# Two gate projections held until a block inversion has ended, its blocks read back over two DMA queues, and a residual scaling moved out of a merge loop

## The chip, the cores and the metric

The program runs on one core of one Trainium2 chip. The metric is the device time of one execution in microseconds. The core has a matrix engine (TensorE, PE in the rows; PEld is its loading of weights), three engines for elementwise work (VectorE or DVE, ScalarE or ACT, GpSimd or POOL), and SyncE (SP), which issues most DMA transfers. Each engine works through its own list of instructions in a fixed order; semaphores hold an instruction back until what it reads has been written.

## The reference, cut to what matters

The reference is three layers with different mixers and a product-key expert layer over 512 tokens of width 1024. The change lies in the third mixer, which runs a stick-breaking attention and a gated delta rule side by side and merges them through two gates:

```python
L = where(strict, einsum('bhnid,bhnjd->bhnij', k_beta, kc) * decay, 0)
T = triangular_solve(eye + L, eye)             # the inverse that the change is about
v_corr = T @ v_beta ; k_cumdecay = T @ (k_beta * exp(gc))
...                                            # scan over the chunks with these
o_gdn = rms_norm(o_gdn, gdn_out_norm_w) * silu(gdn_z)
merged = sigmoid(gate_sb) * y_sb + sigmoid(gate_gdn) * y_gdn
x = x + merged @ w_out
```

`gate_sb`, `gate_gdn` and `gdn_z` are projections of the layer's input. `x` on the last line is the output of a normalisation of the first block, so in the kernel it has still to be scaled by a gain per channel and a factor per token before anything is added to it.

## The kernel before, in words

Activations lie with channels on the 128 partitions and the 512 tokens along the free dimension, as 8 tiles. Every projection is done at nearly float32 accuracy in three products: `weights` (lines 197 to 212) brings a block of 128x1024 weights into `wraw` over the SP queue, ScalarE rounds it into `whi` (L207) and VectorE takes the rest, `wlo` (L208). The pool `wp` has **three buffers for each of `wraw`, `whi` and `wlo`**, shared by all projections. `proj_cols` (L220) then runs 24 matmuls of 512 columns on one PSUM bank of the tag `acc` (two banks): for each k of 8, whi with the high part, whi with the low part, wlo with the high part (L215, L216, L217).

The framework lists the instructions of each engine before the run: whatever is ready and has a free buffer is taken, earlier lines of the program first. Work that is written later thus fills gaps ahead of its place. A dependency of the kind `NoSync` sets this order alone; at run time nothing waits for it.

`gdn` (from L1205) goes through these stages:

- `stage1` for 8 heads makes `U[h]` (the matrices to invert) and stores their 32x32 diagonal blocks in DRAM (`ub`).
- `blocks()` (L1308 to L1320) loads all 128 diagonal blocks at once, one on each partition, inverts them on VectorE in 31 steps of a product (L1317) and a reduction (L1318), and stores them in DRAM (`xb`, L1320).
- `inverse(h)` (L1328 to L1360), run for two heads at a time, brings a head's inverted blocks back into `xd` (the tag `ld`, four buffers) with four DMAs (L1334) after a POOL memset (L1331), and joins them to the full inverse with products on PE (L1344, L1349, L1355, L1358), transposes (L1338, L1352), ScalarE copies (L1347, L1353, L1356) and VectorE operations (L1336, L1339, L1340, L1350, L1359). Its first product, L1344, is ordered behind `beside`, the ScalarE copy of gate tile 8.
- `gate_proj` (L1480) is one of 16 gate tiles (m = 0 to 15): a `proj_cols`, a ScalarE copy into `gp` (L1485) and a store (L1486). Tiles 0 to 8 are written ahead of the `inverse` calls, 9 to 13 between the four rounds of the scan, 14 and 15 behind it.
- `scan` and `finish` go over four rounds of 128 tokens and eight heads; `pair` (L541, its matmuls L556) starts the first two tiles of the next projection with the weights of `br_gdn`.
- `merge` (L1416) takes 8 tiles m: a sigmoid of the gates (L185 from `act`), a POOL product (L1422), the projection `br_gdn` on PE (tiles 2 to 7 in PSUM tag `sc`), a VectorE product and sum (L1425, L1426), the split into `mT` (L191 on ScalarE, L192 on VectorE), and then the scaling of the residual tile `xT[:, m]` (L1429), ordered behind that tile's L1426. The projection `mix_out` follows; its results are added to `xT` (L537).

Of the kernel before, what the change touches and what calls it, by code (L numbers as in the profile page):

```python
# [16 lines left out]
OP = mybir.AluOpType  # L17
AX = mybir.AxisListType
# [122 lines left out]
class Kern:  # L141
# [75 lines left out]
        mm(ps, ll, rh, start=False, stop=stop, **kw)  # L217
        return first

    def proj_cols(self, src, h, tag="acc"):  # L220

        hi, lo = self.weights(src, (8, 128))
        ps = self.ps(tag)
        for k in range(8):
            self.mm3(ps, hi[:, k], lo[:, k], h[0][:, k], h[1][:, k], k == 0, k == 7)
        return ps

    def proj_wide(self, srcs, h, tag="acc"):
# [976 lines left out]
    def gdn(self, ydram, sdram, xdram):  # L1205
# [3 lines left out]
        with ExitStack() as cx:  # L1209
# [99 lines left out]
            def blocks():  # L1309

                UB = p2.tile([128, 1024], F32, name="big", bufs=2).rearrange("p (a b) -> p a b", a=32)
                nc.sync.dma_start(UB, ub.rearrange("u b j i -> (u b) j i"))
                tb = p2.tile([128, 1024], F32, name="big", bufs=2)
                for j in range(30, -1, -1):
                    n = 31 - j
                    t = tb[:, :n * n].rearrange("p (m i) -> p m i", m=n)
                    nc.vector.tensor_mul(t, UB[:, j, j + 1:, None].to_broadcast([128, n, n]), UB[:, j + 1:, j + 1:])  # L1317
                    nc.vector.tensor_reduce(UB[:, j, j + 1:], t.rearrange("p m i -> p i m"), axis=AX.X, op=OP.add,  # L1318
                                            negate=True)
                nc.sync.dma_start(xb.rearrange("u b j i -> (u b) j i"), UB)  # L1320

            def four(fn):
                ps = self.ps("sc", (128, 4, 128))
# [4 lines left out]
            def inverse(h):  # L1328

                xd = p2.tile([128, 4, 128], F32, name="ld", bufs=4)  # L1330
                nc.gpsimd.memset(xd, 0.0)  # L1331
                for b in range(4):
                    r = slice(32 * b, 32 * b + 32)
                    nc.sync.dma_start(xd[r, :, r], xb[4 * h:4 * h + 4, b].rearrange("c j i -> j c i"))  # L1334
                td = p2.tile([128, 4, 128], F32, name="td", bufs=2)
                nc.vector.transpose(td.rearrange("p a b -> p (a b)"), xd.rearrange("p a b -> p (a b)"))  # L1336
                L = p2.tile([128, 2, 4, 128], F32, name="big", bufs=2)
                ps = four(lambda o, c: nc.tensor.transpose(o, U[h][:, c], self.ident))  # L1338
                nc.vector.tensor_mul(L[:, 0], ps, b4(l1))  # L1339
                nc.vector.tensor_mul(L[:, 1], ps, b4(l2))  # L1340
                yield
                P = p2.tile([128, 4, 128], F32, name="P", bufs=2)
                def first(o, c):
                    i = mm(o, L[:, 0, c], xd[:, c], start=True, stop=True)  # L1344
                    tc.add_manual_dep(i.ins, beside, nosync, reason="behind the gates")
                ps = four(first)
                nc.scalar.activation(P, ps, AF.Copy)  # L1347
                yield
                ps = four(lambda o, c: mm(o, td[:, c], P[:, c], start=True, stop=True))  # L1349
                nc.vector.tensor_sub(xd, xd, ps)  # L1350
                yield
                ps = four(lambda o, c: nc.tensor.transpose(o, xd[:, c], self.ident))  # L1352
                nc.scalar.activation(td, ps, AF.Copy)  # L1353
                yield
                ps = four(lambda o, c: mm(o, L[:, 1, c], xd[:, c], start=True, stop=True))  # L1355
                nc.scalar.activation(P, ps, AF.Copy)  # L1356
                yield
                ps = four(lambda o, c: mm(o, td[:, c], P[:, c], start=True, stop=True))  # L1358
                nc.vector.tensor_sub(U[h], xd, ps)  # L1359
                yield  # L1360
# [56 lines left out]
            def merge(p3, R2, ops):  # L1417
                mT = [pool.tile([128, 8, T], F32R, name="mT" + "hl"[z]) for z in range(2)]
                for m in range(8):
                    b, s = ops.pop(0) if ops else operands(p3, m)  # L1420
                    self.act(s, s, AF.Sigmoid)
                    nc.gpsimd.tensor_tensor(b, b, s[:, 0], op=OP.mult)  # L1422
                    ps = first[m] if m < 2 else self.proj_cols(A["br_gdn"][m], yT, "sc")
                    t = p3.tile([128, T], F32, name="mt", bufs=2)
                    nc.vector.tensor_mul(t, ps, s[:, 1])  # L1425
                    after = nc.vector.tensor_add(t, t, b).ins.name  # L1426
                    self.split(mT[0][:, m], mT[1][:, m], t)
                    x = self.xT[:, m]
                    i = nc.vector.scalar_tensor_tensor(x, x, self.fing[:, m:m + 1], R2, op0=OP.mult, op1=OP.mult)  # L1429
                    tc.add_manual_dep(i.ins, after, nosync, reason="behind the merge")  # L1430
                ss, add = self.sums("st")
                self.proj_part(A["mix_out"], rows(mT, 0, 8), self.residual(None, add), "acc", 2,
                               [A["peer_wq"][m] for m in range(2)])
                R = self.sm.tile([128, T], F32, name="R", bufs=1)
                self.rstd = []
                for half, hs in enumerate(HALVES):
                    self.rstd.append(self.rstd_x(ss, half))
                    self.rstd_rows(self.rstd[half], R, hs)
                    self.make_h(R, hs, self.fg)

            blocks()
            for m in range(9):
                beside = self.gate_proj(sdram, pool, m)
            for h in range(0, 8, 2):
                for _ in zip(inverse(h), inverse(h + 1)):
                    pass
# [4 lines left out]
            for c in range(4):  # L1451
                for g in range(4):
                    if g % 2 == 0:
                        raw = p2.tile([128, 4, 128], F32, name="xd", bufs=2)
                        ss = p2.tile([128, 4], F32, name="ss", bufs=3)
                    d = p2.tile([128, 2, 5, 128], F32, name="ld", bufs=4)
                    nc.sync.dma_start(d, gd[c, :, 2 * g:2 * g + 2])
                    for h in range(2):
                        scan(2 * g + h, c, d[:, h], raw, ss)
                    if g % 2:  # L1460
                        old.append((c, g // 2, raw, ss))
                    elif old:
                        finish(*old.pop(0))
                for m in ((9,), (10,), (11, 12), (13,))[c]:
                    self.gate_proj(sdram, pool, m)
            for m in range(14, 16):
                self.gate_proj(sdram, pool, m)
# [9 lines left out]
            nc.sync.dma_start(R2, xdram[:, 8])  # L1477
            merge(p3, R2, ops)

    def gate_proj(self, sdram, pool, m):  # L1480

        w = self.A[("gate_sb", "gate_gdn", "gdn_z")[m // 8]][m % 8]
        ps = self.proj_cols(w, self.hT)
        g = pool.tile([128, T], F32, name="gp", bufs=2)
        i = self.nc.scalar.activation(g, ps, AF.Copy)  # L1485
        self.nc.sync.dma_start(sdram[:, m // 8, m % 8], g)  # L1486
# [334 lines left out]
```

## Time and profile before

| | us |
|---|---|
| median of three runs | 2961.42 (2959.7 to 2961.81) |
| the profiled execution, its own time | 2964.76 |
| its span, first to last instruction | 2963.0 |
| PE busy in the span | 2827.3 (95%) |
| VectorE busy | 2135.7 (72%) |
| ScalarE busy | 1297.6 (44%) |
| POOL busy | 677.8 (23%) |

Times in the rows count from the span's start. In a timeline, a row gives start, duration, engine, line, operation, out<-in, shapes and how often; in brackets stands the idle time of the engine ahead of it and what ended that. An engine name with a q is its sequencer, as when it issues a DMA. The chain of work is followed back from the last instruction, so a stretch that is in it was waited for by what ended last.

### The profile page before, as it was taken

The page shows a single profiled execution, that of the slowest core. Times are in us where ns is not written, and L with a number is a line of the kernel's source. Part 1 is how long each engine was busy: PE and PEld are TensorE (multiplying, and loading weights), DVE is VectorE, ACT ScalarE, POOL GpSimd, SP SyncE. Part 2 cuts the span into 40 slices and gives each one's busy share as a digit, 9 for nine tenths or more (in the row PEclk, how much of TensorE's full clock was granted, in tenths as well). Part 3 has the DMA queues.
Part 4 walks back from the last instruction along what each step waited for, and adds up shares of the span by engine and source line. Part 5 has one row for each costly group of instructions (what it writes and reads, how often), then busy time and mean ns, then how long its engine had stood idle before and what let it go on. Part 6 is the DMA issues. An engine that isn't in the chain of part 4 may idle for free.

```text
span 2963.0 us, 43188 instructions
## 1 busy us (share of the span) xinstructions
PE 2827.3 (95%) x16320; PEld 2478.4 (84%) x16324; DVE 2135.7 (72%) x4184; ACT 1297.6 (44%) x2245; POOL 677.8 (23%) x550
## 2 busy tenths in 40 slices
PE   6999999999999999999889999999999999999989
PEld 5887887888789887777777888998999999999867
DVE  7566456676866554998666888977777777878885
ACT  2222234564755443775353435873333333333323
POOL 0101012110120000111011540005555553333350
PEclk9999999999999999999999999999999999999999
DMA  6453222211131224334363223779888888888773
GB/s 242 135 170 135 73 79 73 68 61 69 48 106 58 82 98 164 117 131 163 106 210 133 83 98 105 220 214 355 306 301 294 299 300 309 307 299 300 272 263 129
DMA packets 201008, 516.62 MB, mean 174 GB/s; under 512 B 27104, under 2 KB 79456, under 8 KB 198496
## 3 DMA queue, kind: packets, MB, share of 16 engines
q1 hardware_dynamic: 163504, 379.36, 37.2%
q0 software_dynamic: 36864, 134.23, 12.4%
q8 instruction: 128, 2.10, 0.3%
q14 instruction: 80, 0.66, 0.1%
q10 hardware_dynamic: 432, 0.27, 0.0%
HBM read 462.15 MB, written 51.64 MB: 173 GB/s over the span
## 4 chain that ended last, share of the span: by engine, by line
PE 69%; DVE 12%; issue 6%; ACT 5%; DMA 4%; POOL 4%; SPq 0%; POOLq 0%; DVEq 0%; ACTq 0%
PE pacc L215 8%; PE pacc L216 8%; PE pacc L217 8%; PE pst L216 5%; PE pst L215 5%; PE pst L217 5%; PE out L216 5%; PE out L217 5%; PE out L215 5%; DVE wlo L208 2%; POOL g L1742 2%; PE pacc L1670 2%; ACT whi L207 1%; PE ptr L1670 1%; DMA g<-in_peer_v_dram,ex 1%
## 5 line engine op out<-in xcount | busy, mean ns | idle before, releaser
L207 ACT ACTIVATE whi<-wraw 128x1024 fp32r<-128x1024 f32 x346 | 364.2, 1054 | 482.4 <-PE pacc L216 213.7
L208 DVE TENSOR_TENSOR wlo<-wraw,whi 128x1024 fp32r<-128x1024 f32 x325 | 407.2, 1254 | 230.8 <-ACT whi L207 225.1
L217 PE MATMUL pst<-hTh,wlo 128*128 128x384 f32 x1024 | 350.2, 342 | 1.7 <-DVE wlo L208 1.7
L215 PE MATMUL pst<-hTh,whi 128*128 128x384 f32 x1024 | 348.6, 340 | 1.0 <-ACT whi L207 1.0
L216 PE MATMUL pst<-hTl,whi 128*128 128x384 f32 x1024 | 348.8, 341 | 0.0
L215 PE MATMUL pacc<-whi,hTh 128*128 128x256 f32 x1216 | 341.0, 281 | 4.5 <-ACT whi L207 1.7
L216 PE MATMUL pacc<-wlo,hTh 128*128 128x256 f32 x1216 | 339.2, 279 | 0.0
L217 PE MATMUL pacc<-whi,hTl 128*128 128x256 f32 x1216 | 339.1, 279 | 0.0
L1742 POOL DMA_INDIRECT g<-in_peer_u_dram,ex x128 | 228.8, 1788 | 402.9 <-DVE w L1768 379.5
L217 PE MATMUL out<-whi,wl 128*128 128x512 f32 x768 | 305.2, 397 | 6.6 <-DVE wl L192 6.6
L216 PE MATMUL out<-wlo,wh 128*128 128x512 f32 x768 | 305.8, 398 | 4.7 <-DVE wlo L208 4.7
L215 PE MATMUL out<-whi,wh 128*128 128x512 f32 x768 | 305.1, 397 | 0.0
L207 ACT ACTIVATE whi<-vr 128x1024 fp32r<-128x1024 f32 x126 | 133.5, 1060 | 275.9 <-PE pst L216 245.7
L1742 POOL DMA_INDIRECT g<-in_peer_v_dram,ex x128 | 180.8, 1412 | 257.7 <-DVE w L1768 230.8
L215 PEld LDWEIGHTS pacc<-whi,hTh 128*128 128x128 f32 x1216 | 228.9, 188 | 5.9 <-ACT whi L207 1.9
L217 PEld LDWEIGHTS pacc<-whi,hTl 128*128 128x128 f32 x1216 | 229.1, 189 | 0.6
L216 PEld LDWEIGHTS pacc<-wlo,hTh 128*128 128x128 f32 x1216 | 228.9, 188 | 0.5
L215 PE MATMUL pacc<-hTh,whi 128*128 128x512 f32 x560 | 221.2, 395 | 1.8 <-DVE old L1132 1.2
L217 PE MATMUL pacc<-hTh,wlo 128*128 128x512 f32 x560 | 221.9, 396 | 0.2 <-DVE wlo L208 0.2
L216 PE MATMUL pacc<-hTl,whi 128*128 128x512 f32 x560 | 221.7, 396 | 0.0
L191 ACT ACTIVATE wh<-w 128x384 fp32r<-128x384 f32 x128 | 67.1, 524 | 340.8 <-PE out L216 274.5
L215 PEld LDWEIGHTS pst<-hTh,whi 128*128 128x128 f32 x1024 | 192.9, 188 | 7.0 <-ACT whi L207 1.3
(646 smaller groups left out, 6551.0 us busy)
## 6 DMA issues: line engine op xcount, KB each, us to landing
wraw<-in_peer_ut_dram SPq DMA_DIRECT2D x128, 512.0 KB
vr<-in_peer_v_dram SPq DMA_DIRECT2D x126, 512.0 KB
gd<-big SPq DMA_DIRECT2D x24, 1024.0 KB
gg<-gd SPq DMA_DIRECT2D x16, 1536.0 KB
wraw<-in_mod_w_dram SPq DMA_DIRECT2D x32, 512.0 KB
wraw<-in_ret_vg_dram SPq DMA_DIRECT2D x32, 512.0 KB
wraw<-in_gdn_qkv_dram SPq DMA_DIRECT2D x24, 512.0 KB
gd<-pk SPq DMA_DIRECT2D x8, 1280.0 KB
```

The costliest lines, as they stand in the source:

```text
L191: nc.scalar.activation(hi, src, AF.Copy)
L207: i = self.nc.scalar.activation(hi, raw, AF.Copy)
L208: j = self.lo.tensor_tensor(lo, raw, hi.bitcast(F32), op=OP.subtract)
L215: first = mm(ps, lh, rh, start=start, stop=False, **kw)
L216: mm(ps, lh, rl, start=False, stop=False, **kw)
L217: mm(ps, ll, rh, start=False, stop=stop, **kw)
L1670: end = mm(ps[:, i], o2[:, i], o1[:, i], start=True, stop=True).ins.name
L1742: i = nc.gpsimd.indirect_dma_start(out=g, out_offset=None, in_=A["peer_u" if up else "peer_v"], in_offset=bass.IndirectOffsetOnAxis(ap=ex[ ...
```

## The change

Four edits, all in `gdn` and its helpers:

- `blocks()` returns the name of its last reduction. `gate_proj` and `proj_cols` take it as `after`: the first matmul of gate tiles 6 and 7 is ordered behind that reduction (NoSync).
- Gate tile 8 is no longer written ahead of the inverses but in the first round of the scan, with 9. `beside` is thereby the copy of tile 7, so L1344 comes behind tile 7.
- Of the four DMAs that bring a head's blocks back, those of b = 0 and 2 are issued from ScalarE's queue, the others from SP's as before.
- In `merge` the scaling of `xT` gets a loop of its own behind the merge loop; `after` is then the sum of tile 7 for all eight.

```diff
-    def proj_cols(self, src, h, tag="acc"):
+    def proj_cols(self, src, h, tag="acc", after=None):
...
-            self.mm3(ps, hi[:, k], lo[:, k], h[0][:, k], h[1][:, k], k == 0, k == 7)
+            m = self.mm3(ps, hi[:, k], lo[:, k], h[0][:, k], h[1][:, k], k == 0, k == 7)
+            if after and k == 0:
+                nosync = mybir.DependencyInfo(mybir.DependencyClass.NoSync, mybir.DependencyReason.SCHED_ONLY)
+                self.tc.add_manual_dep(m.ins, after, nosync, reason="kept for later")
...
-                    nc.vector.tensor_reduce(UB[:, j, j + 1:], t.rearrange("p m i -> p i m"), axis=AX.X, op=OP.add,
-                                            negate=True)
+                    i = nc.vector.tensor_reduce(UB[:, j, j + 1:], t.rearrange("p m i -> p i m"), axis=AX.X, op=OP.add,
+                                                negate=True)
                 nc.sync.dma_start(xb.rearrange("u b j i -> (u b) j i"), UB)
+                return i.ins.name
...
-                    nc.sync.dma_start(xd[r, :, r], xb[4 * h:4 * h + 4, b].rearrange("c j i -> j c i"))
+                    q = nc.sync if b % 2 else nc.scalar
+                    q.dma_start(xd[r, :, r], xb[4 * h:4 * h + 4, b].rearrange("c j i -> j c i"))
...
                     self.split(mT[0][:, m], mT[1][:, m], t)
+                for m in range(8):
                     x = self.xT[:, m]
                     i = nc.vector.scalar_tensor_tensor(x, x, self.fing[:, m:m + 1], R2, op0=OP.mult, op1=OP.mult)
                     tc.add_manual_dep(i.ins, after, nosync, reason="behind the merge")
...
-            blocks()
-            for m in range(9):
-                beside = self.gate_proj(sdram, pool, m)
+            inverted = blocks()
+            for m in range(8):
+                beside = self.gate_proj(sdram, pool, m, inverted if m > 5 else None)
...
-                for m in ((9,), (10,), (11, 12), (13,))[c]:
+                for m in ((8, 9), (10,), (11, 12), (13,))[c]:
...
-    def gate_proj(self, sdram, pool, m):
+    def gate_proj(self, sdram, pool, m, after=None):
...
-        ps = self.proj_cols(w, self.hT)
+        ps = self.proj_cols(w, self.hT, after=after)
```

## Rows read from the trace of the kernel before

**Rows 1.** Waits of PE, 1350 to 1650 us: who, for what, total, times, longest.

```profile
PE psc L1344 <- DMA ld<-xb: 7.6, 1, 7.6
PE psc L215 <- ACT whi L207: 6.5, 1, 6.5
PE pst L1379 <- ACT gvn L1376: 4.5, 10, 1.2
PE psc L1374 <- DVE gsu L1372: 2.4, 6, 0.6
```

**Rows 2.** Stretches: length, busy time of each engine (instructions), PEclk, DMA share, GB/s.

```profile
1378.00:1428.00 50.00, 49.48 (x215) 39.94 (x214) 47.93 (x69) 13.91 (x18) 0.00 (x0) 1.00 0.40 134
...
1560.00:1575.00 15.00, 8.50 (x37) 6.56 (x36) 13.81 (x17) 6.05 (x8) 4.50 (x3) 0.88 0.55 199
1575.00:1595.00 20.00, 19.96 (x79) 15.34 (x79) 12.83 (x15) 8.70 (x11) 3.25 (x2) 0.92 0.39 133
```

**Rows 3.** Chain that ended last, 1340 to 1660 us: start, length, what.

```profile
1424.31 1.21 DVE wlo L208
...
1426.63 1.93 DVE big L1318
...
1435.29 2.05 PE psc L1344 x8
```

**Rows 4.** Line 208 from 1378 to 1430 us: shortest, median, longest ns, first, last.

```profile
L208 DVE TENSOR_TENSOR wlo<-wraw,whi x8: 1202/1216/1220, 1382.0 to 1429.8; 128x1024 fp32r<-128x1024 f32 x8
```

**Rows 5.** Timeline of ScalarE, 1339 to 1545 us.

```profile
1375.28 1.06 ACT L207 ACTIVATE whi<-wraw 128x1024 fp32r<-128x1024 f32 x1 [3.90 <-PE pacc L216]
...
1387.23 0.58 ACT L1485 ACTIVATE gp<-pacc 128x512 f32<-128x512 f32 x1
...
1392.72 0.58 ACT L1485 ACTIVATE gp<-pacc 128x512 f32<-128x512 f32 x1
...
1413.73 1.06 ACT L207 ACTIVATE whi<-wraw 128x1024 fp32r<-128x1024 f32 x1 [3.95 <-PE pacc L216]
...
1437.37 0.60 ACT L1347 ACTIVATE P<-psc 128x512 f32<-128x512 f32 x1 [11.11 <-PE psc L1344]
...
1449.93 0.60 ACT L1347 ACTIVATE P<-psc 128x512 f32<-128x512 f32 x1 [4.24 <-PE psc L1344]
```

**Rows 6.** Timeline of PE, 1435 to 1483 us.

```profile
1436.99 0.77 PE L216 MATMUL pacc<-hTl,whi 128*128 128x512 f32 x1
...
1438.88 1.05 PE L1344 MATMUL psc<-ld,big 128*128 128x128 f32 x8
...
1473.93 0.40 PE L217 MATMUL pacc<-hTh,wlo 128*128 128x512 f32 x1
```

**Rows 7.** A DMA issued by ScalarE (timeline); SP's issues of line 1334, in ns.

```profile
1.16 0.46 ACTq L571 DMA_DIRECT2D R<-in_pos_dram  x1
...
L1334 SPq DMA_DIRECT2D ld<-xb x32: 318/430/432, 1431.5 to 1462.6; - x32
```

**Rows 8.** Chain that ended last, 1562 to 1576 us; line 1429 in ns.

```profile
1563.29 4.81 DVE xT L1429 x4
...
1569.41 0.75 DVE xT L1429
...
L1429 DVE SCALAR_TENSOR_TENSOR xT<-xT,fg,R x8: 739/747/1784, 1563.3 to 1590.4; 128x512 f32<-128x512 f32 x8
```

**Rows 9.** Timeline of PE around the merge's gap, 1540 to 1596 us.

```profile
1567.80 0.39 PE L217 MATMUL psc<-yTh,wlo 128*128 128x512 f32 x1
1574.69 0.80 PE L215 MATMUL psc<-yTh,whi 128*128 128x512 f32 x1 [6.50 <-ACT whi L207]
...
1578.25 0.45 PE L216 MATMUL psc<-yTl,whi 128*128 128x512 f32 x1
```

**Rows 10.** Timelines of VectorE and ScalarE behind tile 6 of the merge.

```profile
1582.46 0.69 DVE L1425 TENSOR_TENSOR mt<-psc,ls 128x512 f32<-128x512 f32 x1 [2.11 <-PE psc L217]
1583.98 0.63 ACT L191 ACTIVATE mTh<-mt 128x512 fp32r<-128x512 f32 x1 [0.69 <-DVE mt L1426]
```

## Prediction, written before the changed kernel ran

> **What bounds the kernel now.** I read three views in order. First PE's waits in the mixer: PE is short of work nearly nowhere, but it stands still twice for long, 7.6 us before L1344 and 6.5 us before tile 6 of the merge, and 6.9 us in small pieces in the scan (4.5 and 2.4) [rows 1]. The change aims at the two long ones. Second the stretches: during the inversion of the blocks PE is full (49.48 of 50.00 us) and VectorE nearly so (47.93); in the stretch of the second gap VectorE has 13.81 of 15.00 us [rows 2]. Third the chain that ended last. Through the inversion it lies on VectorE: reductions L1318 with conversions L208 of gate weights between them, then a store and a load, then L1344 [rows 3]. So the gate tiles that fill PE there are not free: eight conversions of 1.22 us lie between 1382.0 and 1429.8, seven of them ahead of the last reduction [rows 4]. In the merge the chain runs through 4.81 and 0.75 us of L1429 [rows 8].
>
> **The kept tiles: PE.** A gate tile takes 5.49 us of PE, from copy to copy (1387.23 to 1392.72) [rows 5], 0.229 us for each of 24 matmuls. Now the tiles run in order; PE stops inside tile 14, and 38 gate matmuls are left for the stage behind L1344, the first at 1436.99, the last at 1473.93 [rows 6]. With the change PE's list holds tiles 0 to 5, then tiles from 8 on, then 6 and 7, then L1344. The order is set when the program is made; nothing waits for it at run time.
>
> What counts against this is the weights. Nothing holds their preparation back: tile 7's is rounded at 1375.28 [rows 5], tile 6's one tile earlier, and each then keeps one of three buffers of `whi` and `wlo` until its matmuls have run, some 45 us later. Tiles 8, 9 and so on share the third. Today a tile's conversions lie under the matmuls of the tiles before it; with one buffer they stand between tiles: 1.06 us on ScalarE [rows 5] and 1.22 us on VectorE [rows 4], so a period of at least 5.49 + 1.06 + 1.22 = 7.8 us. Above that comes the wait for VectorE, whose list is fixed: the weights rounded at 1413.73 to 1414.79 got their L208 at 1424.31 [rows 3, 5], 9.5 us later. That lag costs nothing now; with one buffer PE stands in it. The lag was not seen in this role, so I bound the period: 7.8 us below, 5.49 + 1.06 + 9.5 = 16 us above. I take 10, nearer the lower end, because the lag builds up only towards the end and a slower PE also spaces the conversions out. From the end of tile 5 (about 1381) to a little before the inversion's end there are 44 us, so 4.4 tiles instead of 8.4. PE loses 4 tiles there, 22 us, against the two tiles (11.0 us) that it does later in a gap of 7.6.
>
> **The kept tiles: L1344.** The last reduction ends at 1426.63 + 1.93 = 1428.56 [rows 3]. Two or three conversions fewer ahead of it make it 1426.1. From its end to L1344 it takes 1435.29 - 1428.56 = 6.7 us. Four issues of 0.43 us stand in that way [rows 7]; over two queues it is two, -0.86. The blocks are then there at 1432.0. PE, though, must first do tiles 6 and 7: I take it that PE comes to them one us ahead of the inversion's end, at 1425.1, and is through at 1436.1, 0.8 us later than L1344 starts today. Two things are better there: the eight instructions of one head's L1344 take 1.05 us at the higher of the two clock levels and took 2.05 behind the gap, at the lower [rows 3, 6], and the 1.9 us of gate matmuls between the two heads, there because the second head's blocks came later [rows 6], go. The second head's L1344 then ends at 1436.1 + 1.9 = 1438.0 against 1438.88 + 0.95 = 1439.8: **-1.8 us**. Bounds: -5.9 if PE is free when the blocks land (1432.0 + 1.9), +6 if PE reaches tile 6 some 8 us later.
>
> **The kept tiles: what is left over.** Of 16 tiles 12.4 are done by then, so 3.6 tiles or 86 matmuls remain, not 38. The inverse stage takes 38 into the holes between its dependent steps, as now; 48, or 11.0 us, go into the scan and ahead of the merge, where PE's small waits are 6.9 us [rows 1]. Filling all of them leaves +4.1, filling none +11; near 0 it is only if the later work that they push on finds room in the merge's gap. I take **+5**: the waits are short (longest 1.2 us), but a gate matmul of 0.229 fits into most of them.
>
> **The second queue.** ScalarE now issues 16 DMAs of about 0.46 us [rows 7], 7 us in all. The first eight fall into 11.11 us in which it is idle, four more into each lull like the 4.24 us before L1347 [rows 5]. The issues wait for the store of the blocks and for the memset of `xd`; queued behind them on ScalarE are the copies of tiles 6 and 7 (each holds one of two `acc` banks) and L1347, for which L1349 waits. Cost **0**; if the eight later ones lie in front of such copies, +3.7 us.
>
> **The scaling behind the merge.** Without 4.81 + 0.75 us of L1429 [rows 8], VectorE is free when tile 5 of the merge ends on PE, at 1567.80 + 0.39 = 1568.2 [rows 9]. From there the present order of ScalarE asks for L1425, L1426, L191 and then the rounding of tile 6's weights: at tile 6 the first three steps take 1583.98 + 0.63 - 1582.46 = 2.15 us [rows 10], then 1.06 for the rounding, 3.2 us in all. PE would go on at 1571.4 instead of 1574.69: -3.3. If the new list puts the rounding ahead of those copies, the gap closes: -6.5. Behind the gap eight matmuls from 1574.69 to 1578.25 take 3.56 us [rows 9] where seven spacings of 0.23 would be 1.6; of these 1.9 us I count half, as a gap of 3.2 us may or may not cost the clock. **-4.2**, bounds -2.5 and -8.4. The eight scalings cost 8 x 0.75 = 6.0 us [rows 8] behind the last sum, where PE has 5.6 us of `mix_out` for each result and VectorE only 12.83 of 20.00 us [rows 2]; the first is needed a tile later. Cost 0; if that cover fails, +2.
>
> **Sum.** -1.8 + 5 + 0 - 4.2 = -1.0 us. The profiled execution took 2964.76 us, 3.3 us more than the median of the runs (2961.42), so the sum goes to the median: **2960 us**. A measurement of this kernel can tell about 0.2%, 5.9 us, from no change.
>
> **Rivals.** (1) *The kept tiles starve nobody* (their weights are prepared late, or a buffer is found). Then L1344 stands at 1432.0 with a full clock (-5.9), no more matmuls are left over than now (0), and the merge gives -4.2: -10.1, **2951 us**; with the merge's gap closed 2947. For it: PE has 7.6 us to fill and the tiles fit. Against it: three buffers, and a preparation that nothing holds. (2) *PE loses its clock between the starved tiles.* Each restart then costs the 1.9 us seen behind the merge's gap, 4.4 times 8.4 us; tiles 6 and 7 stand in PE's list ahead of L1344 and push it to 1444.5. It decides from the point where PE reaches tile 6 later than 1432.0 - 11.0 = 1421.0; each us beyond costs one. 1444.5 + 1.9 - 1439.8 = +6.6, with +5 and -4.2 it is +7.4: **2969 us**. For it: both long gaps were followed by the lower level, 1.2 GHz [rows 3, 6, 9]. Against it: the waits here would be shorter and between them PE works. The Trainium skill (TensorE: Matmul & The Clock Gate, "HAM oscillation — how this bites in real kernels") states that waits between bursts can throttle the engine again before every burst; the two gaps here agree that a wait does it (2.05 us for what takes 1.05), no row here shows it repeated. (3) *The scaling buys nothing* because another step ahead of the rounding on ScalarE is then late: -1.8 + 5 = +3.2, 2964.6 us.
>
> **How the numbers follow.** Forecast 0.32 and rival 3 0.12 both lie within 0.2%: same 0.44, with an own range of 2955 to 2967. Rival 1 0.35, rival 2 0.21. The range goes from the middle of rival 1's two values to rival 2: 2949 to 2969.
>
> **What would show it.** Right: between 1381 and 1425 idle PE ahead of each gate tile, ended by L207 and L208; five or fewer conversions among the reductions; no DMA wait before L1344, its eight instructions at 1.05 us; gate matmuls in the scan; the merge's gap at about 3 us. Wrong: a PE that stays full through the inversion (rival 1), rows of 0.43 us per gate matmul there (rival 2), or a merge gap of 6 us (rival 3). A changed order in later stages, which I hold to be equal, would also break the sum.

## The result, and the profile after

| | before | after |
|---|---|---|
| median of the runs, us | 2961.42 | 2979.05 |
| the profiled execution, its own time, us | 2964.76 | 2974.84 |
| from the inversion's first step to the last sum of `mix_out`, us ("the stage") | 255.7 | 270.1 |

The changed kernel is slower: ratio 1.0059, 95% interval 1.0036 to 1.0081, about 17.5 us. The forecast was 2960 us, with a range of 2949 to 2969. Line numbers move: L1317, L1318 and L1320 of before are L1320, L1321 and L1323 after, L1334 is L1339, L1344 is L1349, L1485 is L1491, L537 is L540.

**Where to measure.** The order of work ahead of the inversion is the same in both programs, yet in the profiled pair it ends 6.4 us later after, and the last 180 us, whose order is the same too, were some 10.5 us longer in the profile of before. Such drift is as large as what is looked for. So each kernel is compared over the stage alone, from the first L1317 to the last L537 in the view of one line (the two numbers behind the comma are the first and the last start). Before:

```profile
L1317 DVE TENSOR_TENSOR big<-big x31: 160/425/1152, 1378.2 to 1425.4; 128x1 f32<-128x1 f32 x1, 128x4 f32<-128x4 f32 x1, 128x9 f32<-128x9 f32 x1, 128x16 f32<-128x16 f32 x1
L537 DVE TENSOR_TENSOR xT<-xT,pacc x10: 420/690/690, 1593.8 to 1633.9; 128x512 f32<-128x512 f32 x6, 128x256 f32<-128x256 f32 x4
L1344 PEld LDWEIGHTS psc<-ld,big x64: 186/192/333, 1435.3 to 1475.0; 128*128 128x128 f32 x64
```

After:

```profile
L1320 DVE TENSOR_TENSOR big<-big x31: 159/424/1161, 1384.6 to 1425.1; 128x1 f32<-128x1 f32 x1, 128x4 f32<-128x4 f32 x1, 128x9 f32<-128x9 f32 x1, 128x16 f32<-128x16 f32 x1
L540 DVE TENSOR_TENSOR xT<-xT,pacc x10: 421/680/689, 1617.3 to 1654.7; 128x512 f32<-128x512 f32 x6, 128x256 f32<-128x256 f32 x4
L1349 PEld LDWEIGHTS psc<-ld,big x64: 186/192/338, 1436.1 to 1474.7; 128*128 128x128 f32 x64
```

1633.9 - 1378.2 = 255.7 us before, 1654.7 - 1384.6 = 270.1 after: +14.4. By parts: from the start of the inversion to the first product 57.1 and 51.5 us (-5.6), from the first to the last product of the inverse 39.7 and 38.6 (-1.1), from there to the last sum 158.9 and 180.0 (+21.1). So the inverse is ready 6.7 us sooner, and all is lost behind it.

What PE waited for, 1350 to 1680 us after (compare [rows 1]), line 208 from 1384 to 1436 us (one conversion where [rows 4] has eight), the stretch of the inversion (columns as in [rows 2]), and ScalarE's timeline there ([rows 5]):

```profile
PE pacc L215 <- ACT gp L1491: 36.3, 1, 36.3
PE psc L215 <- ACT whi L207: 3.2, 1, 3.2
```

```profile
L208 DVE TENSOR_TENSOR wlo<-wraw,whi x1: 1218/1218/1218, 1388.4 to 1388.4; 128x1024 fp32r<-128x1024 f32 x1
```

```profile
1384.40:1434.40 50.00, 13.90 (x61) 11.08 (x59) 44.95 (x69) 1.97 (x3) 0.00 (x0) 0.67 0.17 54
```

```profile
1387.12 1.06 ACT L207 ACTIVATE whi<-wraw 128x1024 fp32r<-128x1024 f32 x1 [3.95 <-PE pacc L216]
1388.09 0.58 ACT L1491 ACTIVATE gp<-pacc 128x512 f32<-128x512 f32 x1
1430.82 2.78 ACTq L1339 DMA_DIRECT2D ld<-xb  x6
1433.98 0.60 ACT L1491 ACTIVATE gp<-pacc 128x512 f32<-128x512 f32 x1 [45.31 <-DMA ld<-xb]
1434.06 0.85 ACTq L1339 DMA_DIRECT2D ld<-xb  x2
```

PE ran 61 matmuls in 50 us where it ran 215. The wait of 7.6 us is not filled, it has grown to 36.3 us. The profile puts that down to a copy of a gate tile, and ScalarE's row says why the copy is late: six block loads stand ahead of it in ScalarE's list and wait until 1430.82 for the store of the blocks. That reading, the obvious one, is wrong as the cause, as the first experiment shows.

The PE timeline has the two facts that the cause is made of:

```profile
1397.91 0.40 PE L217 MATMUL pacc<-hTh,wlo 128*128 128x512 f32 x1
1434.63 0.80 PE L215 MATMUL pacc<-hTh,whi 128*128 128x512 f32 x1 [36.33 <-ACT gp L1491]
1435.22 0.63 PE L216 MATMUL pacc<-hTl,whi 128*128 128x512 f32 x1
1435.65 0.63 PE L217 MATMUL pacc<-hTh,wlo 128*128 128x512 f32 x1
1436.07 0.63 PE L215 MATMUL pacc<-hTh,whi 128*128 128x512 f32 x1
1436.50 3.02 PE L1349 MATMUL psc<-ld,big 128*128 128x128 f32 x16
```

Tile 7, the second of the tiles that were to be kept, ends at 1398.3, 30 us ahead of the inversion's end: nothing held it. And between its end and the first product of the inverse only four gate matmuls stand in PE's order. In the unbroken run of gate matmuls ahead of the first product the program has 270 before and 120 after.

The wait in the merge is the one of [rows 9], on the same timeline; the eighth matmul behind it is the last to start at the longer spacing:

```profile
1595.72 0.79 PE L215 MATMUL psc<-yTh,whi 128*128 128x512 f32 x1 [3.19 <-ACT whi L207]
...
1599.23 0.40 PE L216 MATMUL psc<-yTl,whi 128*128 128x512 f32 x1
```

### The profile page after: what moved, and what is told of

It is laid out like the page before. It is cut to its first block, busy times and chain, and to the rows that moved or that the text cites. A ratio compares the mean times of both kernels' runs of the same rounds, so it can differ in the third digit from the quotient of the medians.

```text
span 2973.0 us, 43188 instructions
## 1 busy us (share of the span) xinstructions
PE 2824.2 (95%) x16320; PEld 2478.7 (83%) x16324; DVE 2133.3 (72%) x4184; ACT 1297.7 (44%) x2245; POOL 666.2 (22%) x550
## 4 chain that ended last, share of the span: by engine, by line
PE 75%; DVE 11%; ACT 4%; issue 4%; DMA 3%; POOL 2%; SPq 0%; ACTq 0%; POOLq 0%; DVEq 0%
PE pacc L215 8%; PE pacc L216 8%; PE pacc L217 8%; PE pst L216 6%; PE pst L215 6%; PE pst L217 6%; PE out L216 6%; PE out L217 6%; PE out L215 6%; PE pacc L1676 2%; DVE wlo L208 2%; PE ptr L1676 1%; ACT whi L207 1%; DVE big L1321 1%; DVE cv L1249 1%
## 5 line engine op out<-in xcount | busy, mean ns | idle before, releaser
L208 DVE TENSOR_TENSOR wlo<-wraw,whi 128x1024 fp32r<-128x1024 f32 x325 | 408.0, 1257 | 242.1 <-ACT whi L207 238.8
L207 ACT ACTIVATE whi<-wraw 128x1024 fp32r<-128x1024 f32 x346 | 363.9, 1054 | 460.4 <-PE pacc L216 198.3
L215 PE MATMUL pst<-hTh,whi 128*128 128x384 f32 x1024 | 348.4, 340 | 1.0 <-ACT whi L207 1.0
L215 PE MATMUL pacc<-whi,hTh 128*128 128x256 f32 x1216 | 341.5, 281 | 3.4 <-ACT whi L207 1.7
L215 PE MATMUL out<-whi,wh 128*128 128x512 f32 x768 | 304.2, 396 | 0.8 <-ACT wh L191 0.8
L215 PE MATMUL pacc<-hTh,whi 128*128 128x512 f32 x560 | 222.5, 397 | 38.0 <-ACT gp L1491 36.3
L207 ACT ACTIVATE whi<-vr 128x1024 fp32r<-128x1024 f32 x126 | 133.5, 1060 | 271.9 <-PE pst L216 245.7
L215 PEld LDWEIGHTS pacc<-whi,hTh 128*128 128x128 f32 x1216 | 229.3, 189 | 4.8 <-ACT whi L207 1.9
L1748 POOL DMA_INDIRECT g<-in_peer_v_dram,ex x128 | 174.2, 1361 | 255.8 <-DVE w L1774 232.0
L191 ACT ACTIVATE wh<-w 128x384 fp32r<-128x384 f32 x128 | 67.1, 524 | 334.9 <-PE out L216 270.8
L215 PEld LDWEIGHTS pst<-hTh,whi 128*128 128x128 f32 x1024 | 192.8, 188 | 7.0 <-ACT whi L207 1.3
```

What stands on the lines that cost most here:

```text
L191: nc.scalar.activation(hi, src, AF.Copy)
L207: i = self.nc.scalar.activation(hi, raw, AF.Copy)
L208: j = self.lo.tensor_tensor(lo, raw, hi.bitcast(F32), op=OP.subtract)
L215: first = mm(ps, lh, rh, start=start, stop=False, **kw)
L1748: i = nc.gpsimd.indirect_dma_start(out=g, out_offset=None, in_=A["peer_u" if up else "peer_v"], in_offset=bass.IndirectOffsetOnAxis(ap=ex[ ...
```

## Experiments

Two theories. **Q**: ScalarE's waiting block loads hold the copies of tiles 6 and 7, PE has no free bank. **H**: the hold leaves PE's list without work between tile 7 and the first product; whoever is named as the releaser, there is nothing to run. The table gives, for each kernel, the gate matmuls ahead of the first product in the program, PE's longest wait in the inversion, the first product after the inversion's start, the stage, and the ratio of times where it was timed against before. A stage is read from one profile: from the first to the last product of the inverse, where before, the scaling moved and the last two rows have the same lists, it takes 39.7, 40.8, 39.7 and 40.9 us. So a difference of about 1 us between two stages shows nothing by itself.

| kernel | matmuls | PE's wait, us | first product, us | stage, us | ratio (95%) |
|---|---|---|---|---|---|
| before | 270 | 7.6 | 57.1 | 255.7 | |
| changed | 120 | 36.3 | 51.5 | 270.1 | 1.0059 (1.0036 to 1.0081) |
| changed, one queue | 120 | 34.9 | 49.4 | 269.6 | 1.0051 (1.0031 to 1.0071) |
| before, two queues | 265 | 8.8 | 57.1 | 257.3 | 1.0004 (0.9995 to 1.0013) |
| before, scaling moved | 270 | 7.6 | 57.0 | 254.6 | 0.9996 (0.9985 to 1.0007) |
| changed, no hold | 265 | 9.1 | 57.4 | 255.6 | 0.9991 (0.9977 to 1.0004) |
| held 12 and 13 of 14 | 264 | 8.2 | 56.3 | 254.1 | |
| held 9 of 10 | 169 | 27.0 | 52.7 | 260.0 | |
| held 6 and 7 in `sc` | 163 | 22.7 | 55.1 | 264.7 | |
| `wlo` on POOL | 241 | 22.3 | 60.8 | 258.6 | 1.0041 (1.0025 to 1.0057) |
| 16 tiles ahead | 308 | under 1 | 58.1 | 253.7 | 0.9990 (0.9981 to 0.9999) |
| 16 ahead, merge reordered | 308 | under 1 | 57.9 | 246.2 | 0.9968 (0.9956 to 0.9980) |
| merge reordered alone | 270 | 7.6 | 57.0 | 250.6 | 0.9981 (0.9971 to 0.9991) |
| the same, scaling moved | 270 | 8.0 | 57.5 | 249.3 | 0.9972 (0.9961 to 0.9983) |

**The changed kernel with one queue.**

```diff
-                    q = nc.sync if b % 2 else nc.scalar
-                    q.dma_start(xd[r, :, r], ...)
+                    nc.sync.dma_start(xd[r, :, r], ...)
```

> The changed kernel with all block loads back on SP. The stage, from the first step of the inversion on VectorE to the last sum of mix_out, took 255.7 us before and 270.1 after; PE stood still 36.3 us in it. Theory Q (ScalarE's issues of block loads wait for the inversion and hold the copies of tiles 6 and 7 behind them, so PE finds no free bank): the copies run at once, the 36 us go, stage about 252 us (the merge's gain stays), time about 2957 us. Theory H (holding two tiles empties PE's list: only four gate matmuls stand there between the end of tile 7 and the first product of the inverse, and held or not they are over at once): PE still idles 33 to 38 us, now until the blocks have landed, stage 266 to 271 us, time 2972 to 2980 us.

PE's waits in this kernel, ScalarE's timeline, and PE's:

```profile
PE psc L1348 <- DMA ld<-xb: 34.9, 1, 34.9
```

```profile
1394.77 0.58 ACT L1490 ACTIVATE gp<-pacc 128x512 f32<-128x512 f32 x1
1431.91 0.60 ACT L1351 ACTIVATE P<-psc 128x512 f32<-128x512 f32 x1 [36.57 <-PE psc L1348]
```

```profile
1394.52 0.40 PE L215 MATMUL pacc<-hTh,whi 128*128 128x512 f32 x1
1429.83 2.47 PE L1348 MATMUL psc<-ld,big 128*128 128x128 f32 x9 [34.92 <-DMA ld<-xb]
```

The copy of tile 7 runs at once, at 1394.77, the bank of tile 7 is free from 1395.35, tile 8 has begun in the other, and PE still stands for 34.9 us, now until the blocks land. Stage 269.6 and time fall into H's bounds (stage 266 to 271, ratio 1.0051). Q is out as the cause of the loss: ScalarE's wait of 45.3 us was real, but it only hid that there was nothing to release. Where the queue shows is the first product: 49.4 us here, 51.5 with two queues. There the blocks come a little sooner (the two heads' transposes start 2.5 and 3.4 us behind the first issue, at 1433.27 and 1434.20 against 1430.80; with one queue 3.2 and 5.0 us, at 1429.82 and 1431.64 against 1426.62), but PE has four gate matmuls ahead of the product, and these wait for the late copy and then run at the lower clock (the last three 0.43 us apart, where it is 0.23 at the higher one).

**The queue alone.**

```diff
-                    nc.sync.dma_start(xd[r, :, r], ...)
+                    q = nc.sync if b % 2 else nc.scalar
+                    q.dma_start(xd[r, :, r], ...)
```

> The kernel before with only the block loads b = 0 and 2 moved to ScalarE. Theory Q: ScalarE stands over 30 us at its first block load, PE likewise; stage 265 to 270 us, time about 2975 us. Theory H: the list of PE is full up to the end of the inversion, the issues stand late in ScalarE's list and at most one copy behind them; PE's gap ahead of the first product 5 to 9 us (7.6 before), stage 254 to 257 us, time 2956 to 2966 us.

Stage 257.3 us, 0.3 above H's bound and far from Q's; time 1.0004. The issues (the timeline of before with one queue has `1431.46 7.50 SPq L1334 DMA_DIRECT2D ld<-xb  x16`):

```profile
1442.23 4.96 ACTq L1335 DMA_DIRECT2D ld<-xb  x8
1442.39 5.77 SPq L1335 DMA_DIRECT2D ld<-xb  x8
...
1446.37 2.04 PE L1345 MATMUL psc<-ld,big 128*128 128x128 f32 x8 [8.82 <-DMA ld<-xb]
1447.31 0.60 ACT L1486 ACTIVATE gp<-pacc 128x512 f32<-128x512 f32 x1 [15.75 <-DMA ld<-xb]
```

The sixteen issues are over after 5.9 us (1442.23 to 1448.16) instead of 7.5. They are not slower one by one (median 0.39 us on either queue, 0.43 before), but both queues stand in the middle, SP from 1443.24 to 1445.47 and ScalarE from 1444.50 to 1445.60. What held them was not found; in the changed kernel two queues issue together without such a hole, 8 in 3.71 us and 6 in 2.78. The first head's product starts 4.14 us behind the first issue (1446.37 - 1442.23); before, it was 3.83 (1435.29 - 1431.46). Only one gate copy stands behind ScalarE's issues here, and it is not among what PE waited for. Nothing is won; the stage is 1.6 us longer, within the 3.7 that the prediction gave as its bound.

**The scaling alone.**

```diff
                     self.split(mT[0][:, m], mT[1][:, m], t)
+                for m in range(8):
                     x = self.xT[:, m]
```

> The kernel before with only the scaling in a loop of its own behind the merge. My forecast for this part: PE's gap in the merge 3.2 us (6.5 before), stage 255.7 - 4.2 = 251.5 us, time about 2957 us. Rival: the gap stays above 6 us because another step is late, stage 255.7 us, 2961 us.

Neither: the wait is 4.3 us and the stage 254.6, a gain of 1.1 us. The merge itself gains more: from the first matmul of its projection (L215 on `yTh`) to the last sum it takes 93.2 us (1541.6 to 1634.8) where before took 95.5 (1538.4 to 1633.9), about the 2.2 us by which the wait is shorter; the inverse ahead of it, with the same list, was 1.1 us longer in this profile. VectorE, ScalarE and PE at the wait:

```profile
1571.50 0.69 DVE L1425 TENSOR_TENSOR mt<-psc,ls 128x512 f32<-128x512 f32 x1 [1.54 <-PE psc L217]
1572.11 1.36 DVE L192 TENSOR_TENSOR mTl<-mt,mTh 128x512 fp32r<-128x512 f32 x1
1573.39 0.68 DVE L1426 TENSOR_TENSOR mt<-mt,ld 128x512 f32<-128x512 f32 x1
```

```profile
1574.10 0.63 ACT L191 ACTIVATE mTh<-mt 128x512 fp32r<-128x512 f32 x1 [2.52 <-DVE mt L1426]
1574.64 1.04 ACT L207 ACTIVATE whi<-wraw 128x1024 fp32r<-128x1024 f32 x1
```

```profile
1575.73 0.70 PE L215 MATMUL psc<-yTh,whi 128*128 128x512 f32 x1 [4.34 <-ACT whi L207]
...
1579.29 0.40 PE L216 MATMUL psc<-yTl,whi 128*128 128x512 f32 x1
```

L192 of the tile before comes between L1425 and L1426, 1.3 us that the forecast's 3.2 did not have (in the changed kernel it does not come there, and the wait is 3.2). The eight scalings, 8 x 0.7 us behind the last sum, delay nothing: from the third result of `mix_out` on VectorE waits 2.8 us for most of them. The restart is paid in full: seven steps in 3.56 us here (1575.73 to 1579.29) as behind the longer wait of before. What makes PE wait is that L207 stands behind L191 in ScalarE's list; with the scaling gone the way to L191 is shorter, the order is the same.

**The changed kernel without the hold.**

```diff
-                beside = self.gate_proj(sdram, pool, m, inverted if m > 5 else None)
+                beside = self.gate_proj(sdram, pool, m, None)
```

> The changed kernel without the hold: tiles 6 and 7 run when they can, all else of the change stays (two queues, tile 8 in the scan, the scaling behind the merge). Theory H: no gap of over 9 us on PE, stage 250 to 253 us, time about 2957 us. Theory Q: the gap of over 30 us stays, stage 266 to 270 us, time about 2973 us.

The wait is 9.1 us, the stage 255.6, the ratio 0.9991. The 36 us go with the hold alone, which is H's second half. The stage is 2.6 us over H's upper bound, which counted 4.2 us for the scaling: alone it gave 1.1 of stage, and the stage with two queues alone is 1.6 longer.

**The hold at another place.** Held tiles 12 and 13, with 14 tiles written ahead of the inverse and one queue:

```diff
-            for m in range(8):
-                beside = self.gate_proj(sdram, pool, m, inverted if m > 5 else None)
+            for m in range(14):
+                beside = self.gate_proj(sdram, pool, m, inverted if m > 11 else None)
```

> The changed kernel with one queue, but 14 tiles are written ahead of the inverse and the held ones are 12 and 13. Theory H, place decides: PE's list then has 264 gate matmuls up to the first product of the inverse, against 270 before and 120 in the changed kernel; no gap of 30 us, the one ahead of the first product 8 to 10 us, stage 253 to 257 us, time about 2960 us. Rival, the hold as such costs (a held tile keeps a bank and a weight buffer wherever it lies): gap well over 10 us, stage over 260 us.

Wait 8.2, stage 254.1: as with the scaling moved and no hold. A hold costs by its place, not by itself. The dose between, one held tile, number 9 of ten (one queue; tile 9 is no longer called in the scan):

```diff
-            for m in range(8):
-                beside = self.gate_proj(sdram, pool, m, inverted if m > 5 else None)
+            for m in range(10):
+                beside = self.gate_proj(sdram, pool, m, inverted if m > 8 else None)
```

> One held tile, number 9, of ten written ahead, one queue, the scaling behind the merge: PE's list has 169 gate matmuls up to the first product, 101 fewer than before. Theory H with a price by the count: PE is through with them 101 x 0.229 = 23 us earlier than before, first product some 52 us after the inversion's start (about three conversions are left among the reductions), gap ahead of it 24 to 27 us, stage 254.5 + 15.1 x 101 / 150 = 264.7 us, time about 2970 us. Rival, by my forecast's step: with one held tile two weight buffers stay free and PE goes on through later tiles, gap under 12 us, stage about 256 us.

```profile
PE psc L1348 <- DMA ld<-xb: 27.0, 1, 27.0
```

The wait is 27.0 us, at the upper end of H's bounds, and the step of the forecast ("PE goes on through later tiles") is refuted again, with one tile held in place of two. And here a bank is free: the copy of tile 8 runs at 1403.14, the weights of tiles 10 and 11 are converted among the reductions (1399.99 and 1407.85), and still only five matmuls of tile 10 stand ahead of the product, behind tile 9. The stage, 260.0, is 4.7 us less than the price by the count: 101 matmuls, 23.1 us of PE, cost 5.4 us over the 254.6 of the scaling alone, the next 49 (11.2 us) cost 9.6. The first ones find room, since the first product comes 4.3 us sooner and the scan's small waits take them: L1379's 4.5 us of [rows 1] are 0.8 in the changed kernel and nothing here; in the changed kernel PE was busy 56.24 of 60 us from 1485 to 1545 (53.93 of 62 us from 1482 to 1544 before). Once these are full, a matmul costs nearly its length, by these three runs; the next one, with 163 matmuls, does not fit the count.

**The held tiles in other banks.** Tiles 6 and 7 in PSUM tag `sc`, one queue:

```diff
-        ps = self.proj_cols(w, self.hT, after=after)
+        ps = self.proj_cols(w, self.hT, "sc" if after else "acc", after=after)
```

> The changed kernel with one queue, its held tiles 6 and 7 in banks of the tag sc instead of acc, so that both acc banks stay free: 163 gate matmuls stand ahead of the first product (120 in the changed kernel, 270 before). If the banks are what let no later tile pass the held ones (and the weight buffers, that I took for the limit, only stop the list some 40 matmuls later): gap 25 to 29 us instead of 34.9, stage 259 to 262 us (the run with 169 ahead had 27.0 and 260.0). Rival, nothing passes the held tiles whatever their bank: gap about 35 us, stage 268 to 271 us.

The wait falls to 22.7 us, below the bounds given: with other banks for 6 and 7, tiles 8 and 9 do pass them, and no more. The stage is 264.7 all the same, between both expectations. What appears now is what the forecast had feared for the changed kernel:

```profile
1387.10 0.50 PE L215 MATMUL pacc<-hTh,whi 128*128 128x512 f32 x1 [0.92 <-ACT whi L207]
...
1388.36 0.50 PE L217 MATMUL pacc<-hTh,wlo 128*128 128x512 f32 x1 [0.53 <-DVE wlo L208]
...
1394.60 0.50 PE L215 MATMUL pacc<-hTh,whi 128*128 128x512 f32 x1 [0.91 <-ACT whi L207]
...
1397.26 0.50 PE L217 MATMUL pacc<-hTh,wlo 128*128 128x512 f32 x1 [1.93 <-DVE wlo L208]
```

With two weight buffers kept, a tile begins 7.5 us after the one before (1387.10, 1394.60) and PE waits at its start for L207 and then L208, 4.3 us for two tiles. From 1399.12 to 1402.39 its matmuls are 0.43 us apart, the lower clock that rival 2 had in mind. ScalarE's and VectorE's timelines at the end of the wait:

```profile
1415.92 0.58 ACT L1490 ACTIVATE gp<-psc 128x512 f32<-128x512 f32 x1
1438.43 0.60 ACT L1490 ACTIVATE gp<-pacc 128x512 f32<-128x512 f32 x1 [21.93 <-DMA sd<-gp]
```

```profile
1435.32 0.71 DVE L1340 STREAM_TRANSPOSE td<-ld 128x512 f32<-128x512 f32 x1 [5.96 <-DMA ld<-xb]
...
1437.88 0.65 DVE L1343 TENSOR_TENSOR big<-psc,l 128x512 f32<-128x512 f32 x1
```

The copy of tile 8, whose matmuls were over at 1393.7, stands in ScalarE's list behind those of 6 and 7 (`gp<-psc`), so `acc` has no free bank for tile 10. The first product, at 1438.74, is 2.4 us later than with tile 9 held, but the blocks are not: they are read 3.3 us after the first of their loads was issued (1432.04). The product also needs L1343, and that stands in VectorE's list behind the transposes of the blocks and a conversion, where with one queue alone it follows the last reduction at once (1423.94).

**The conversions off VectorE.** The changed kernel's one gain was an inversion with one conversion in place of seven (43.5 us to the last reduction's end, 50.3 before). To have it with PE full, `wlo` of the gate tiles is made on POOL, which is idle there ([rows 2]); scaling behind the merge:

```diff
+        self.lo = self.nc.gpsimd
         ps = self.proj_cols(w, self.hT)
+        self.lo = self.nc.vector
```

> The kernel before with the scaling behind the merge, and the second half of the weights (wlo) of the 16 gate tiles made on POOL instead of VectorE. If the conversions among the reductions are what the inversion pays for its fillers: inversion 50.3 - 7 x 1.22 = 41.8 to 43.5 us, first product at about 50 us, 29 gate matmuls fewer ahead of it; they cost about 4 us later, stage about 252 us, time 2958 us. Rival, POOL and VectorE hold each other up when both work: reductions or conversions take longer, inversion stays above 47 us, stage 255 us or more.

The rival holds, and more than it asked for: inversion 55.0 us, stage 258.6, ratio 1.0041. The stage is only part of that loss: about 10 us lie ahead of it. From the first L1295 on POOL, in `stage1`, to the inversion's first step it takes 182.9 us (1212.1 to 1395.0) where before took 173.2 (1205.0 to 1378.2); conversions of the first gate tiles stand there in POOL's list between the products of `stage1`. This part was not taken apart. VectorE's groups in the inversion, before (1378 to 1429 us) and then here (1395 to 1451 us; count | busy us, mean ns | idle before):

```profile
L1318 DVE TENSOR_REDUCE big<-big 128x1 f32<-128x1 f32 (+30 forms) x31 | 25.4, 818 | 1.0
L1317 DVE TENSOR_TENSOR big<-big 128x1 f32<-128x1 f32 (+30 forms) x31 | 15.8, 509 | 1.5 <-DMA big<-ub 0.6
L208 DVE TENSOR_TENSOR wlo<-wraw,whi 128x1024 fp32r<-128x1024 f32 x7 | 8.5, 1213 | 0.0
```

```profile
L1317 DVE TENSOR_TENSOR big<-big 128x1 f32<-128x1 f32 (+30 forms) x31 | 28.1, 905 | 16.5 <-DMA big<-ub 15.5
L1318 DVE TENSOR_REDUCE big<-big 128x1 f32<-128x1 f32 (+30 forms) x31 | 24.8, 801 | 1.1
```

The products with two inputs took 12.3 us more, the reductions with one input nothing. One conversion ran on POOL from 1422.94 for 2.41 us:

```profile
1423.39 2.52 DVE L1317 TENSOR_TENSOR big<-big 128x529 f32<-128x529 f32 x1
1425.95 1.38 DVE L1318 TENSOR_REDUCE big<-big 128x23 f32<-128x529 f32 x1
1427.36 0.76 DVE L1317 TENSOR_TENSOR big<-big 128x576 f32<-128x576 f32 x1
```

**All gate tiles ahead.** What would fill the 7.6 us without a hold: the 38 matmuls that now run between the products of the inverse.

```diff
-            for m in range(9):
+            for m in range(16):
                 beside = self.gate_proj(sdram, pool, m)
```

(The calls for tiles 9 to 15 further down go; the scaling is moved.)

> The kernel before with the scaling behind the merge and all 16 gate tiles written ahead of the inverse, no hold: 308 gate matmuls stand ahead of the first product, none behind it. If the 38 that ran in the holes of the inverse delayed its products: gap of 7.6 us filled, first product at about 58 us (57.0 before), the inverse 35 to 38 us long (40.1 before), stage about 252 us, time 2958 us. Rival, they were free there, and PE now loses its clock in the holes: inverse 40 us or more, stage 255 us or more, time 2961 us or more.

The wait is gone, the first product at 58.1 us as worked out, the inverse from first to last product 38.3 us long (39.7 before), between the two bounds. Against the scaling alone it is 0.9 us of stage, which is not told from nothing. The 38 matmuls were nearly free where they were; there was no 7.6 us to be won.

**The order in the merge.** From the reading of the scaling run: write the projection of tile m + 1 ahead of the sums of tile m, so that its L207 comes ahead of L191.

```diff
+                nxt = first[0]
                 for m in range(8):
+                    ps = nxt
+                    if m < 7:
+                        nxt = first[1] if m < 1 else self.proj_cols(A["br_gdn"][m + 1], yT, "sc")
                     b, s = ops.pop(0) if ops else operands(p3, m)
...
-                    ps = first[m] if m < 2 else self.proj_cols(A["br_gdn"][m], yT, "sc")
```

With the 16 tiles ahead and the scaling moved:

> All 16 gate tiles ahead of the inverse, the scaling behind the merge, and in the merge the projection of tile m + 1 written ahead of the sums of tile m, so that ScalarE rounds its weights ahead of the copies of the splits. If the rounding's place in ScalarE's list is what is left of the gap in the merge (4.3 us): gap under 1.5 us, no restart at the lower clock (1.7 us), stage 253.7 - 4.5 = 249 us, time 0.15 to 0.3% below the kernel before. Rival, VectorE's sums are late anyway and the gap only moves to a later tile: stage 252 us or more, time 0.1% below as with the 16 tiles alone.

Wait in the merge gone, stage 246.2 us (2.8 less than expected), ratio 0.9968 (0.9956 to 0.9980): faster than both kernels, 9.5 us by the ratio. The order by itself on the kernel before, and with the scaling:

> The kernel before with one edit: in the merge the projection of tile m + 1 is written ahead of the sums of tile m, the scaling stays in the loop. If the place of the rounding in ScalarE's list makes PE's gap in the merge and the scaling only lengthens the way to it: gap 0 to 2 us with the scaling still in the loop, no restart, stage 255.7 - 7 = 248 to 250 us, time about 0.25% below. Rival, VectorE's scaling makes the gap (the theory behind the part of the change in the merge): gap 4 us or more, stage 253 us or more.

> The same edit and the scaling behind the merge. If the order does it all: stage and time as with the order alone, within 1.5 us. Rival, the scaling is worth something of its own once the order is right: stage 2 to 4 us shorter than with the order alone.

Alone 250.6 us, 0.6 over its bound; with the scaling 249.3, which is within the 1.5 us of "the order does it all". The stages mislead here: up to the merge both kernels have the same list, and the profile with the scaling is 1.6 us longer there. From the first L215 on `yTh` to the last sum it is 90.5 us with the order alone (1544.5 to 1635.0) and 87.5 with both (1544.0 to 1631.5), so 3 us less, as the rival had it. By time (0.9981 and 0.9972, with intervals that overlap) the two are not told apart. VectorE and ScalarE with the order alone (L1432 is the scaling there):

```profile
1569.37 3.78 DVE L1432 SCALAR_TENSOR_TENSOR xT<-xT,fg,R 128x512 f32<-128x512 f32 x4
```

```profile
1569.58 1.04 ACT L207 ACTIVATE whi<-wraw 128x1024 fp32r<-128x1024 f32 x1
1574.57 0.63 ACT L191 ACTIVATE mTh<-mt 128x512 fp32r<-128x512 f32 x1 [3.95 <-DVE mt L1429]
```

Four scalings still stand in VectorE's way, 3.78 us, and L191 waits 3.95 us for it, but L207 has run beside them and PE loses nothing by it but 1.6 us of another wait. So the long wait in the merge was made by ScalarE's order, and the scaling set its length. With the order right, the scaling still seems to cost about 3 us in the loop, 1.6 of which is the wait named; the rest was not traced.

## Why the prediction was wrong

The step that failed is the sentence "With the change PE's list holds tiles 0 to 5, then tiles from 8 on, then 6 and 7". It holds tiles 0 to 7 in their old order and four matmuls of tile 8: 120 ahead of the first product instead of 270, and PE stands 36.3 us. Nothing passes the held tiles. That the hold does it, and that its place counts, is shown: without it the wait is 9.1 us, with a late one 8.2. Why nothing passes is shown in part. The prediction asked only for the weights, though it knew the banks (it names them under the second queue); with the held tiles in other banks, 43 more matmuls pass and the wait is 22.7 us instead of 34.9. But that both `acc` banks belong to the held tiles cannot be all of it: with one tile held, one bank was free and nothing passed either. A rule that a tile gets its buffer only after every earlier tile has got its own would fit both this and the late copy of tile 8 in the run with other banks; no run tests it. And "I take it that PE comes to them one us ahead of the inversion's end" stands two paragraphs behind the remark that nothing waits for the order at run time. Tiles 6 and 7 ran as early as before, and the list behind them was empty.

Point by point:

- *PE loses 4 tiles, 22 us,* and does two of them later, so 48 matmuls or 11.0 us net. It lost 150 matmuls, 34.4 us.
- *L1344, -1.8, bound -5.9.* Counted from the inversion's start the second head's product ends at 54.9 us (1436.50 + 3.02) and did at 61.7 (1438.88 + 1.05, [rows 6]): -6.8. One conversion of `wlo` is left in the inversion where there were seven, not five. The direction was right, the size past its bound. (For the end before, the prediction adds 0.95 us where the row has 1.05.)
- *Left over, +5.* 188 matmuls remained instead of 86. From the last product to the last sum it took 21.1 us more. This term is the loss. That some of the work finds room in the scan was right: 34.4 us cost 15.0 over the whole stage (269.6 against 254.6, both with one queue and the scaling moved).
- *The second queue, 0, upper bound +3.7.* 1.6 us of stage on the order of before, 0.5 with the hold, and no change of time (1.0004): right by size. The remark on the copies queued behind ScalarE's issues came true at its worst, 45.3 us, and cost nearly nothing, as PE had nothing to run.
- *The merge, -4.2.* The wait of 3.2 us in the changed kernel is exactly the one worked out. The restart was counted at half, and is paid whole behind 3.2, 4.3 and 6.5 us alike: in the changed kernel seven steps take 3.5 us (1595.72 to 1599.23), where 1.6 would be seven of 0.23. Alone, with its wait of 4.3, the part is worth 2.3 us in the merge, just short of the bound of 2.5, 1.1 us of stage and 0.04% (-0.07 to 0.15) of time, not to be told from nothing.
- *The scaling's own cost, 0.* Right.
- *Rival 2, 2969 us by starved tiles and a restart each.* Nearest in time, and not what happened: PE stood once, for want of work; starved tiles and the lower clock among them were seen only with the held tiles in other banks, 4.3 us of waits for two tiles. That the time came out nearest to this rival is chance. *Rival 1*, that nobody starves and L1344 gains 5.9, had this gain and not its price: PE did not stay full.

## What to carry to other kernels

Before an order is costed, ask what the engine's list can hold between the moved work and its new place: work that is put back can keep all that stands behind it from passing, by its output banks as well as by its weights, and in one run here though a bank was free. An order without a wait changes the list and not the time: work that can start early does, and the hole moves behind it. And the engine that the profile names as the releaser of a long wait is the last of several: take it away in one run before the loss is laid to it; the same 35 us were put down to a copy with two queues and to a DMA with one.

## What the runs showed of the hardware

- VectorE's products with two inputs stretched while POOL converted: 28.1 us for what took 15.8, 2.52 us for a product of 529 elements where one of 576 without POOL beside it took 0.76; reductions were not touched (24.8 and 25.4). The Trainium skill (SBUF — State Buffer, "SBUF: two separate sides") says that VectorE and GpSimd share one pair of ports that one of them holds for a whole instruction, among others where a VectorE operation with two SBUF inputs meets a GpSimd operation that reads SBUF; the trace agrees.
- ScalarE stood 45.3 us at a DMA issue that waited for data, with two ready copies behind it. The Trainium skill (TensorE: Matmul & The Clock Gate, "Architectural detail: the array is 16× 32×32, not 1× 128×128") calls the queues of ACT and DVE strict FIFO; the trace agrees, and the issue of a DMA counts.
- Sixteen block loads were issued in 7.5 us on one queue and in 5.9 on two, in a run where both queues stood for 1.1 and 2.2 us between issues of 0.39 us; the first head's product was not sooner there (4.14 against 3.83 us behind the first issue). The Trainium skill (DMA: Bandwidth & Descriptors, "Issuing engines are not separate DMA queues") states that issuing from several engines saves only the time of the issue; the trace agrees as far as it goes, 1.6 us were saved there.
